# One-level Strassen products for the mLSTM branch and the output projection of a hybrid mLSTM / attention layer

## The chip, the cores and the metric

The kernel runs on one core of a Trainium2 chip. TensorE (PE in the profile) multiplies matrices, VectorE (DVE) and ScalarE (ACT) do element work and read its results from PSUM, GpSimd (POOL) does element work between SBUF tiles, and SyncE's queue (SP) issues most of the DMAs. The metric is the device time of one execution in microseconds (us), the median of several runs. Lower is better.

## The reference

One layer of a diffusion backbone in float32, with 1024 latent tokens of width 1024 and 256 context tokens. Two token mixers work on the same modulated input: windowed attention and a bidirectional mLSTM. Their outputs `att` and `ml` (1024x1024 each) are merged, projected and added to the input; a convolutional feed-forward network (FFN) follows. The part that the change touches:

```python
def merge_branches(att, ml, ga_pre, gm_pre, w_branch_att, w_branch_ml, w_out):
    y = jax.nn.sigmoid(ga_pre) * (att @ w_branch_att) + jax.nn.sigmoid(gm_pre) * (ml @ w_branch_ml)
    return y @ w_out
...
    acc = conv_b
    for j in range(CONV_W):
        acc = acc + up[:, j:j + L] * conv_w[j]
    a, g = jnp.split(acc, 2, axis=-1)
    return (jax.nn.silu(g) * a) @ w_down
```

There are three products of 1024x1024 by 1024x1024 here: the attention branch, the mLSTM branch and the output projection. Behind the projection stand a gated residual, a norm, and the up projection `h @ w_up` of the FFN.

## The kernel before

**Precision.** Every float32 matrix product is made of three fast passes. An operand `x` is split into a high part (a copy to `float32r`, on ScalarE) and a low part (`x - high`, on VectorE); `split_from` (line 47) does both. `mm3` (line 85) and `product` (line 1897) then issue high x high, high x low and low x high for each block of 128 along the contraction. A tile of 128x512 of a 1024-deep product is so 8 x 3 = 24 matmuls of 512 columns.

**Stages.** `layer_kernel` (line 100) runs the startup, the attention with its gate projections (`stage_attention`, line 518), the mLSTM (`stage_mlstm`, line 906), and the tail (`stage_tail`, line 1583), which calls `stage_ffn` (line 2018).

**The order.** In the attention and the mLSTM the order of the instructions is written out by hand. `Pinned` (line 494) chains the instructions of each of PE, DVE, ACT and POOL in the order in which they are emitted; all of them show line 504 in the profile. `ORDER_CORE` (line 885) is a string in which each letter takes the next step of one generator in `stage_mlstm`: for instance `m` is a step of the output gates, `D` and `O` are state updates and outputs, `N` loads an operand of the attention branch, `X` and `Z` make its high and low parts, `Y` is one block of its product (3 matmuls), and `l` multiplies a finished tile by its gate. Half of the attention branch (8 of 16 tiles, 64 `Y`) is done here, in `att_step` (line 1544). In the tail nothing is pinned: the framework's scheduler orders each engine's instructions by their place in the program and by what is ready in its own model of time.

**The tail.** In this order:

- the other 8 tiles of the attention branch (`ya`), with the loads and splits of `mT`, the mLSTM's output, beside them (`ml_load`, `ml_split`, lines 1666 and 1671); gated results go to `y1_d` in DRAM
- the mLSTM branch: 16 tiles `ym` of 24 matmuls. Each is multiplied by its gate (line 1711), the attention branch is added (line 1712), and the sum `y` is split for the next product. Beside them run 16 of the 64 steps of the modulation (`mod_product`, line 201, and `mod_row`, line 223; the first 48 ran in the attention stage, at one or two per block of queries)
- the output projection: 16 tiles `op` in `project` (line 1734), added into the residual `acc` on VectorE. `weight_sums` (line 1815) makes the first 5 of 11 sums of the down projection's weights on VectorE beside it. With the projection's second half the input of the up projection is made: squares and factors of the norm, `first_half` (line 1773) transposes the first 512 tokens, and `pair_sums` (line 1786) makes Strassen operands from the others
- the up and the down projection as Strassen products already, in units (`Units`, line 1906) and in 7 products

GpSimd has only the norm factors to do in the tail. PSUM has 8 banks, in pools with tags, of which the next free one is given.

Of the kernel before, what the change touches and what calls it, by code (L numbers as in the profile page):

```python
# [8 lines left out]
F32 = mybir.dt.float32  # L9
# [90 lines left out]
def layer_kernel(ctx: ExitStack, tc: tile.TileContext, A: dict, out: bass.AP, dbg=None):  # L100
# [25 lines left out]
    ps1 = psx.enter_context(tc.tile_pool(name="ps_mm", bufs=2, space=PSUM, reuse_waits="tile"))  # L126
    pst = psx.enter_context(tc.tile_pool(name="ps_tp", bufs=3, space=PSUM, reuse_waits="tile"))
# [10 lines left out]
    def mm_tile(name):  # L138
        return ps1.tile([P, 512], F32, tag="mm", name=name)

    def fl_tile(name):
        return ps1.tile([P, 512], F32, tag="fl", name=name, bufs=1)

    def tp_tile(name):
        return pst.tile([P, 512], F32, tag="tp", name=name)

    def s_tile(name):
# [6 lines left out]
        nc=nc, tc=tc, A=A, ident=ident, expo=expo, vecT=vecT, mods=mods, m2=m2, g_d=g_d, wmod={}, maccs={}, rows=[], hT=hT, gtile=gtile, gb=gb, dr=dr, out=out,  # L154
        attT_d=attT_d, mlT_d=mlT_d, sga_d=sga_d, sgm_d=sgm_d, kx_d=kx_d, vx_d=vx_d, sil3=sil, sil=sil[:, :, 0], dbg=dbg,
        mm_tile=mm_tile, fl_tile=fl_tile, tp_tile=tp_tile, s_tile=s_tile, psx_s=psx_s,
# [21 lines left out]
    E.ph1, E.sX = ph1, ExitStack()  # L178
    with ExitStack() as st:
        stage_mlstm(E, st)  # L180
    if "mlT" in dbg:
        dump(nc, tc, mlT_d, dbg["mlT"])
# [6 lines left out]
    E.sX.close()  # L189
# [11 lines left out]
def mod_product(E, pool, n):  # L201


    nc, (i, k) = E.nc, divmod(n, KT)
    q, o = i // 2, i % 2 * 4
    if k == 0:
        E.macc = pool.tile([P, 512], F32, tag="macc", name=f"macc{i}", bufs=1 if q < 3 else 2)
        E.maccs[i] = E.macc
    ws, bufs = E.wmod, 1 if q < 3 else 3
    for m in range(n, min(n + bufs, 48 if q < 3 else 64)):  # L210
        if m not in ws:
            ws[m] = pool.tile([P, 512], F32, tag="wmod", name=f"wmb{m}", bufs=bufs)
            nc.sync.dma_start(ws[m], E.A["w_modB"][m // KT][:, m % KT])
    w = ws.pop(n)
# [4 lines left out]
    if k == KT - 1 and q < 3:  # L219
        E.rows.append(i)  # L220


def mod_row(E, pool, i):
# [8 lines left out]
    if i in (1, 7):  # L232
        pg = E.tp_tile(f"gT{q}")
        nc.tensor.transpose(pg[:KT, :P], E.m2[:, 0], E.ident)
        row = pool.tile([P, 512], F32, tag="wmod", name=f"grow{q}", bufs=1 if q < 3 else 3)[:KT, :P]
        nc.vector.tensor_copy(row, pg[:KT, :P])
        nc.sync.dma_start(E.g_d[q // 3].rearrange("o (k c) -> (o k) c", c=P), row)
# [280 lines left out]
def stage_attention(E, st, at):  # L518
# [306 lines left out]
    for n in range(N + 6):  # L825
        a, s, c, x, y = [Bs.get(n - d) for d in (0, 1, 3, 4, 5)]
        quota = (0, 0, 4)[n] if n < 3 else (7 if n < N else 10)
        for step in ORDER if n < N else ORDER_END:
# [37 lines left out]
            elif step == "p" and n < N and mods.n < 3 * (n + 1) // 2:  # L866
# [19 lines left out]
    "vEvvvEvevvUvUvuEvuKvVveEwvvvUKAvuvVvBAvevwBqqKVqeqwwqwAqkkBHDDHmcUqzUqAzqcQuquyqqBqqqqSSQSSymmsmmsmhmmhSaSMSaSEmmsmmsh"  # L886
    "EmDeDammUcmUcmh1mumCu1mMaEmCmdemdmmEmDMDemcUmcUmumCmumCdOeIdOmmfmmMgmGmmDFIDcUmfmcUmMumCgmCmOdFIdOumfmmgmmMmFImDfDmcUm"
    "gUmCmcmFmMdOCuIAuOdmfmBmmAmgmvMBDFGIDUcvfcUvCuvCgvAvdFOdIBODfDuUvgUvAcvFcKIVuvCuvfwvCdvgvdvFBvvKvVvwvOIO1vf1vgvviIvKrv"
    "fvpVDgDvUiUvRvcvwvCcvuKdOVIuCO1wvfd1vgvviIvrvfpvgDDKVvUiUvRvcvwCcvuvCdvuOdIO1vf1xvgKvVviIwvrvfpvgvvivRKvVvwAOIO1xBvf1v"
    "AgvvivBIrqKfpqVqgAqRqwBqTiTwtqPwrqrPqrqprqtqpRQqApqyqRpRqBPkQkRPmHmyTHzPmmtzmTPSStSSSSsSSsmhmsmhmamMmhsmEmamhmamEmaemm"  # L890
    "mEDDmcmcUmMmUemuEmummmMmemDDmcUemcUmu1mum1mCmMmdGmmmDDmcUmCUmuMmdCmcmOdIMuOCmfmdmgmmmDFIDcUmfmcUCmgmMmCdOAFIuOdmfBmmAm"
    "gmvMBDGFIDUcvfUcvCuvCgvAvdFOuIBODfDdUvgUvAcvFcIKVvuCuvfwvCdvgvvdFvuBvKvVOwIOvfvgvvFIvfvDgDKVvUcUvwFvCcvuCvdOuIdO1vf1vg"
    "vviKIVvfwvDgDvUiUvcvcvCuCvudOIKdVO1vfw1vgvviIvfvDgDvUiUvcvcKvVuvCuCwvdOIdO1vf1xvgvviIvKVvfwvAgvviAOBIO1xvfB1vvgqKiVqwI"
    "rPqwrwqprqrpqARkpfmRmrBmprmDRrpDRqHgpqAqipQzTrTRUqtRUqRtpyqPcqRqcPuquBqPkQTPTHyStSSzStmmsSSsShSmhammsmMEmsmhmamhmameED"
    "aDmcmUmcmUmu1mMum1CmECmdmMmdemEDDmcemcmUmUmumCuOMIdGOmmmmmmfDCDgMmUmeUmcmFdIcmmuOummfmCmgMmCmDdFIdOUcDfmumUCgmmmdmMFcI"
    "OAummfmBCmmAmgvMDBGDFIUOcUvdvcvfuvuAgvCDBDCFIOUdfUvcvgAvdvKFVcICOuvfwCvdvgvdvFuIBvfvKvgVvwOFIO1vf1vgvviIvrvfpDKDVgvUvi"
    "UvRvcvwCcvuOCdIO1uvfd1vgKvVviIwvrvfpDDgvUviUvRvcKvcVuvCwCOdIO1dvfuvgvviIvrvfpvKVgvvivRvwvvOIKVOvfwvgvAviIvABvrvBfvpqgK"
    "VqRqwqiqrPqApTrTBkrPDrRDqpctcqHpqRtzqpQRqUyqURqPuuqPqqPkQTTHyStSSzStmmsSSsShSmhammsmNmsDhDamUhmUcmMNmcmCumCamDdDNmUcmU"
    "amnCmdMINdOOfcmnumCgImbmufDFdDumUcmbUmgOMmCcmFIdOCumfumdDDgmUmUcmFIcOMumfumCmgCmDdDFIcOUdmfUmcCmgmCmmMdFIuOdmfmnuDgDnm"
    "UcmUIcFOCumfumnCdmbmgnmMDbdDFIcUOcmfmuCmgCmbmmdbFIdOMmfDDgmmmimcIOcCmmfdCNgXXNiIMZNOXZfNZXYNgXYXNiYXZNIXOdYNfZXYZNXYgY"  # L900
    "NXiYXZIOZNYXZfYNZXYNgYNiYXZINXOZYfNZYXngYXYniXZIOXZYfZYbgYbYiIZrYZrYNplrYNlrpYfRYprlrYRprgYXYpRXYRpiYZrTpZTNtYpRtYNRRY"
    "RYZYXZTXZTYtlYtZYYYlYYYYYYYYlYYYYYYYYlYYYYYYYl"
# [3 lines left out]
def stage_mlstm(E, st):  # L906
# [5 lines left out]
    psd = E.psx_s.enter_context(tc.tile_pool(name="ps_d", bufs=2, space=PSUM, reuse_waits="tile"))  # L912
# [11 lines left out]
    zz = mp.tile([P, P], F32, name="zz")  # L924
    nc.gpsimd.memset(zz, 0.0)
    ones = mp.tile([P, P], F32, name="onesm")
    nc.gpsimd.memset(ones, 1.0)
# [3 lines left out]
    def gate_math():  # L931
        with ExitStack() as s2:
# [4 lines left out]

            lf = gp.tile([P, NBLK, 8], F32, name="lf")
# [384 lines left out]
    def update():  # L1323
        for h, d, i in STEPS:
            c = chunk(d, i)
            (kh, kl), (vh, vl) = kw.pop((h, d, i)), V[h, c]
            dC[h, d, i] = pd = psd.tile([P, 512], F32, tag="d", name=f"dC{h}_{d}_{i}")
# [158 lines left out]
    E.y1_d = dr.tile([D, L], F32, name="y1_d")  # L1486
    E.aT, E.wba = [[], []], []
    araw, ag, psy = {}, {}, {}

    def x512(pool, name, dt=F32R):  # L1490
        return E.xts[pool].tile([P, 512], dt, tag="x", name=name)

    def att_load():
        for q in range(24):
            k, a = (q // 2, q % 2) if q < 16 else (q - 16, 2)
            if q == 4:
                E.ph1.close()
                E.xts = [E.sX.enter_context(tc.tile_pool(name=f"xt{i}", bufs=8, reuse_waits="tile")) for i in range(6)]
            if q < 4 or q >= 16:
                raw = wp.tile([P, 4, P], F32, tag="ub", name=f"ar{q}", bufs=4).rearrange("p c t -> p (c t)")  # L1500
            else:
                raw = x512(5, f"ar{q}", F32)
            if a == 0:
                nc.sync.dma_start(raw, A["w_ba"][0][:, k])
            else:
                nc.sync.dma_start(raw, E.attT_d[0][k * P : (k + 1) * P, (a - 1) * 512 : a * 512])
            araw[q] = raw
            yield

    def att_high():  # L1510
        for q in range(24):
            k, a = (q // 2, q % 2) if q < 16 else (q - 16, 2)
            to = E.wba if a == 0 else E.aT[a - 1]
            pool_ = ((3, 4), (0, 1), (2, 5))[a][k // 4]
            to.append([x512(pool_, f"a{a}{x}{k}") for x in "hl"])
            copy(to[-1][0], araw[q])
            yield

    def att_low():
        for q in range(24):  # L1520
            k, a = (q // 2, q % 2) if q < 16 else (q - 16, 2)
            hi, lo = (E.wba if a == 0 else E.aT[a - 1])[k]
            sub(lo, araw.pop(q), hi)
            yield

    def att_place(c):
        return sl(c % 4 * P, P), sl(c // 4 * 512, 512)

    def att_gate_load():
        for c in range(8):  # L1530
            if c % 2 == 0:
                i = bs.take(("g", c // 2), 2)
                for j, x in enumerate("hl"):
                    ag[c + j] = bp.tile([P, 512], F32, tag=f"b{x}{i}", name=f"sga{c + j}")
            rs, ts = att_place(c)
            nc.sync.dma_start(ag[c], E.sga_d[rs, ts])
            yield

    def att_gate():
        for c in range(8):  # L1540
            act.activation(ag[c], ag[c], AF.Sigmoid)
            yield

    def att_step():
        for k, c in [(k, c) for k in range(KT) for c in range(3)] + [(k, c) for c in range(3, 8) for k in range(KT)]:
            if k == 0:
                psy[c] = bk.take(("y", c), f"ya{c}")
            mm3_step(psy[c], cols(E.wba[k], sl(c % 4 * P, P)), E.aT[c // 4][k], k == 0, k == KT - 1)
            yield

    def att_out():
        for c in range(8):
# [745 lines left out]
```

## Time and profile before

| what | us |
|---|---|
| runs shown: median of 3 | 1937.71 |
| lowest and highest | 1933.21, 1939.3 |
| the profiled execution's own time | 1932.65 |
| its span, first to last instruction | 1930.6 |
| first matmul of the attention branch, from the start | 1005.0 |
| first matmul of the mLSTM branch | 1101.8 |
| first matmul of the output projection | 1196.8 |
| first matmul of the up projection | 1292.7 |

The page begins with the busy time of each engine and its share of the span. A digit in its 40 slices is the busy share in tenths. In a view by windows, a row gives the window, its length, then for each engine the busy time and the number of instructions, then the granted share of TensorE's clock, the busy share of the DMA engines and GB/s. In a view of one tile, a row gives an operation, how often it ran, its shortest, median and longest time in ns, and when the first and the last one started. In a timeline, the first number is the start and the second the duration, both in us. Matmuls overlap in TensorE, so that a row's duration is longer than the time from one start to the next.

### The profile page before, as it was taken

The numbers are of one execution on the slowest core, as the hardware profiler recorded it, in microseconds if no ns is written. First come the engines' busy times: TensorE is split into PE (matmuls) and PEld (weight loads), VectorE is DVE, ScalarE is ACT, GpSimd is POOL, SyncE is SP. The second block draws the span as 40 slices with busy tenths as digits, with TensorE's granted clock in tenths as the row PEclk, the third lists the DMA queues.
The fourth block names the chain that finished last, engine by engine and source line by source line (L and its number), as shares of the span: only waits on it lengthen the run. The fifth ranks groups of instructions, "written<-read, shape, count | busy, mean of one in ns | idle before, by whom it ended". The sixth has DMA issues, their size and how long they took to land.

```text
span 1930.6 us, 28360 instructions
## 1 busy us (share of the span) xinstructions
PE 1902.0 (99%) x10108; PEld 1644.5 (85%) x10108; DVE 1352.8 (70%) x2642; ACT 963.4 (50%) x1897; POOL 346.9 (18%) x594
## 2 busy tenths in 40 slices
PE   8999999999999999999999999999999999999998
PEld 3988888888888899999997787887888888888887
DVE  2877767777776456666585467369878898895564
ACT  4856556556556354646354322256545444465441
POOL 1333333333333133434321000010000000000000
PEclk9999999999999999999999999999999999999999
DMA  8723223223222321413238667622244544499641
GB/s 313 231 93 94 77 66 104 72 77 91 80 67 74 103 62 51 117 49 99 55 122 277 219 201 238 231 88 81 94 151 187 196 153 174 164 326 326 230 164 66
DMA packets 134062, 273.34 MB, mean 142 GB/s; under 512 B 14736, under 2 KB 47136, under 8 KB 130592
## 3 DMA queue, kind: packets, MB, share of 16 engines
q1 hardware_dynamic: 127392, 256.85, 40.1%
q10 hardware_dynamic: 5760, 10.49, 1.7%
q0 software_dynamic: 768, 4.20, 1.3%
q8 instruction: 79, 1.29, 0.3%
q14 instruction: 63, 0.52, 0.1%
HBM read 201.67 MB, written 74.00 MB: 143 GB/s over the span
## 4 chain that ended last, share of the span: by engine, by line
PE 89%; DVE 4%; DMA 3%; ACT 2%; issue 1%; POOL 1%; SPq 0%; ACTq 0%; POOLq 0%; DVEq 0%
PE g L504 9%; PE kv L504 7%; PE pq L504 6%; PE mo L504 5%; PE pa L1901 4%; PE pa L1902 4%; PE pa L1903 4%; PE s L504 4%; PE po L504 4%; PE pt L504 3%; PE q L504 2%; PE ya L504 2%; PE dx L1901 2%; PE dx L1903 2%; PE dx L1902 2%; PE pb L1901 2%
## 5 line engine op out<-in xcount | busy, mean ns | idle before, releaser
L504 DVE CUSTOM_DVE_ANT_0 P<-s,maskA,nsink 128x640 f32<-128x640 f32 (+1 forms) x112 | 103.5, 924 | 76.8 <-PE s L504 75.2
L504 ACT ACTIVATE P<-P,st 128x640 f32<-128x640 f32 (+1 forms) x128 | 102.4, 800 | 87.9 <-DVE st L504 87.8
L504 ACT ACTIVATE ph<-pt 128x512 fp32r<-128x512 f32 x152 | 90.4, 598 | 60.0 <-PE pt L504 58.4
L504 DVE TENSOR_TENSOR pl<-pt,ph 128x512 fp32r<-128x512 f32 x152 | 101.1, 681 | 25.8 <-ACT ph L504 25.6
L504 POOL TENSOR_SCALAR P<-P,st 128x640 f32<-128x640 f32 (+1 forms) x128 | 110.9, 886 | 32.0 <-DVE st L504 11.1
L504 PE MATMUL g<-hH,fh 128*128 128x512 f32 x256 | 106.5, 416 | 0.2 <-ACT fo L504 0.2
L504 PE MATMUL g<-hH,fl 128*128 128x512 f32 x256 | 100.9, 394 | 0.0
L504 PE MATMUL g<-hL,fh 128*128 128x512 f32 x256 | 100.8, 394 | 0.0
L504 PE MATMUL pt<-ident,P 128*128 128x128 f32 x608 | 90.9, 272 | 0.5 <-DVE m L504 0.5
L504 PE MATMUL pq<-w1h,hH 128*128 128x384 f32 (+1 forms) x256 | 87.1, 340 | 0.0
L504 PE MATMUL kv<-w1h,hH 128*128 128x384 f32 x256 | 86.9, 340 | 0.0
L504 PE MATMUL pq<-w1l,hH 128*128 128x384 f32 (+1 forms) x256 | 86.9, 339 | 0.0
L504 PE MATMUL pq<-w1h,hL 128*128 128x384 f32 (+1 forms) x256 | 86.5, 338 | 0.0
L504 PE MATMUL kv<-w1h,hL 128*128 128x384 f32 x256 | 86.1, 336 | 0.0
L504 PE MATMUL kv<-w1l,hH 128*128 128x384 f32 x256 | 86.1, 336 | 0.0
L504 PEld LDWEIGHTS pt<-ident,P 128*128 128x128 f32 x608 | 75.4, 140 | 12.2 <-DVE m L504 0.7
L504 PE MATMUL mo<-w1h,hH 128*128 128x256 f32 x256 | 72.5, 283 | 0.0
L504 POOL TENSOR_SCALAR ss<-ss 128x5 f32<-128x5 f32 x64 | 13.2, 206 | 327.1 <-DVE ss L504 324.1
L504 PE MATMUL mo<-w1h,hL 128*128 128x256 f32 x256 | 71.8, 281 | 0.0
L504 PE MATMUL mo<-w1l,hH 128*128 128x256 f32 x256 | 71.7, 280 | 0.0
L49 DVE TENSOR_TENSOR dfl<-drf,dfh 128x512 fp32r<-128x512 f32 x55 | 38.0, 691 | 46.1 <-ACT dfh L44 46.1
L2039 ACT ACTIVATE cv<-ua,vecT 128x1024 f32<-128x1024 f32 x22 | 27.4, 1245 | 85.5 <-DVE ua L2012 85.5
(581 smaller groups left out, 6346.6 us busy)
## 6 DMA issues: line engine op xcount, KB each, us to landing
ur<-in_w_up SPq DMA_DIRECT2D x22, 1024.0 KB, 5.0
wmb<-in_w_modB SPq DMA_DIRECT2D x64, 256.0 KB, 2.8
f_d<-cv SPq DMA_DIRECT2D x22, 512.0 KB, 2.7
wm<-in_w_modA SPq DMA_DIRECT2D x16, 512.0 KB, 8.2
fr<-in_w_g SPq DMA_DIRECT2D x32, 256.0 KB, 2.7
drf<-fs_d SPq DMA_DIRECT2D x15, 512.0 KB, 5.8
drw<-wt_d SPq DMA_DIRECT2D x14, 512.0 KB, 5.6
w1b<-in_w_cx SPq DMA_DIRECT2D x16, 388.0 KB, 5.1
```

The source lines that it names most:

```text
L49: (nc.vector if eng == "v" else nc.gpsimd).tensor_tensor(lo, src, hi.bitcast(F32), op=ALU.subtract)
L504: i = f(*a, **k)
L1901: nc.tensor.matmul(ps, lh, rh, start=start and i == 0, stop=False, skip_group_check=True)
L1902: nc.tensor.matmul(ps, lh, rl, start=False, stop=False, skip_group_check=True)
L1903: nc.tensor.matmul(ps, ll, rh, start=False, stop=stop and i == n - 1, skip_group_check=True)
L2039: nc.scalar.activation(r, u, AF.Identity, bias=vecT[:, V_CB + ch : V_CB + ch + 1], scale=cw(1))
```

## The change

The mLSTM branch and the output projection become Strassen products: both matrices are cut into quadrants of 512x512, and 7 products of half size, of sums and differences of quadrants, take the place of 8. All three merges, and the up projection up to its first unit's first matmuls, are put in the written order: `stage_tail` starts behind them.

- `merge_steps` makes lists of steps under letters, and `ORDER_CORE` and the new string `ORDER_MERGE` take them in turn. A product step `5` is 6 matmuls (2 blocks of the contraction, one bank of 128x512); 4 banks and 2 steps each make one of the 7 products. The attention branch keeps its plain form (`Y`, 128 steps, 46 of them in `ORDER_CORE`).
- Operands are held in tiles of 128x1024 (`Gen`: a list of slots in three pools). `2` loads one, `X` makes a high part (ScalarE), `Z` a low part (VectorE), `4` a sum on GpSimd, a backquote a sum on VectorE, `3` scales a weight of the output projection by the residual's gate (VectorE).
- Partial results move from PSUM to `U` and `U4` tiles (`#` on ScalarE; `$`, `%`, `(`, `)`, `*` on VectorE), are gated (`9`, VectorE) and added to the attention branch (`~`, now on GpSimd). In the output projection, `&` adds such a tile into the residual on GpSimd and `^`, `(`, `)`, `*` add the last product from PSUM on VectorE.
- The first five weight sums (`[` loads, `]` sums) go from VectorE to GpSimd.
- The 16 late modulation steps go into the attention stage, at two per block instead of one or two.
- All loads of the stage go through SP's queue; gates and `y1` went through ScalarE's before.
- PSUM banks are named one by one (`bank`) instead of given by pools, and `lead` no longer splits the first up unit.

The core of the diff:

```diff
-            elif step == "p" and n < N and mods.n < 3 * (n + 1) // 2:
+            elif step == "p" and n < N and mods.n < min(2 * (n + 1), 64):
...
+ORDER_MERGE = (
+    "8888YY27YlY2YY2YXY2YZXY6Y2lXYZY6XY2ZY7Y2ZXYY27YZYX2lYYZX6Y2YZXY2YZY72YlY`6YYYY4Y7YlYY64Y`YYY7YYlYY6XYY2ZYYX2YY7l2YZY2Y"
+    "Y`6YYYY4lY7Y6YY4Y`Y7YYlYY6YYYY7YYlYY6XY2YXZY2YZ7Y25lX25ZX652ZX45`75[ZX45`#52Z#45`#5`#2X3542Z5352]35X2]35Z]5$4X5$$5ZX[]"
+    "5$Z52X35]Z5]X[35X9]Z5]9529]XZ5[X]95Z~5Z~563X8]536X85ZX]7%5~X%5Z7~6%58X]%[Z5]67Z58X]Z5]Z75X]5X(Z]5X(X5]X9(5](Z5~Z569458"
+    "995Z75~Z5)~6)589~6)58)~67589467589579~57~5`68~5`685*4X6`85X0Z757Z075*0`50*5X*0X95Z0~#5Z05909~#59#5#~X5~XZ5ZX45X`5XZ45Z"
...
+SUMS = dict(m="DPPDPDDP", o="DPDPPDPP")
+YADD = "PPPP"
...
+    def split(key, src, last):
+        def high():
+            h = gs.tile((key, "h"), nm(key) + "h")
+            T[key] = h, gs.tile((key, "l"), nm(key) + "l")
+            act.activation(h, T[src], AF.Copy)
+
+        def low():
+            dve.tensor_tensor(T[key][1], T[src], T[key][0].bitcast(F32), op=ALU.subtract)
...
+    def summ(q, i, out, a, b, alu, rel=()):
+        eng = SUMS[q][i]
+        op("4" if eng == "P" else "`", lambda: (pool if eng == "P" else dve).tensor_tensor(T[out], T[a], T[b], op=alu), rel)
...
+    def wsum(k, j):
+        (a0, a1), (b0, b1) = [[T["w", k, x][:, i * 512 : (i + 1) * 512] for i in range(2)] for x in range(2)]
+        o, a, b = ((a0, a1, a0), (a1, b1, a1), (b1, b1, a0), (b0, b0, b1))[j]
+        pool.tensor_tensor(o, a, b, op=ALU.subtract)
...
+    OPS = {1: ("A11", "B11"), 6: ("S2", "T2"), 2: ("A12", "B21"), 5: ("S1", "T1"), 7: ("S3", "T3"), 3: ("S4", "B22"), 4: ("A22", "T4")}
...
+        def prod(p, banks, start):
+            def step(z, c):
+                if start and z == 0:
+                    ps[q, p, c] = E.bank(banks[c], f"{q}p{p}_{c}")
+                o = ps[q, p if start else {2: 1, 3: 5, 4: 7}[p], c]
+                a, b = [T[q, "p" + x, z] for x in OPS[p]]
+                lhs, rhs = [part(a, kk, sl(c * P, P)) for kk in Z2], [part(b, kk, full) for kk in Z2]
+                product(fixed, o, lhs, rhs, start and z == 0, z == 1)
...
+        def pre(b, h, u):
+            pool.tensor_tensor(acc[b][:, h], acc[b][:, h], u(), op=ALU.add)
...
-            dv = nc.vector.tensor_tensor(sg, ps, sg, op=ALU.mult)
-            nc.vector.tensor_tensor(sg, sg, y1, op=ALU.add)
...
+                (dve if YADD[c] == "D" else pool).tensor_tensor(o, sg.pop(key), y1.pop(key), op=ALU.add)
...
     scale(4)
-    U.lead(0)
     U.prep_apart(0, lambda n, dt=F32R: x512(n, dt, 1))
     scale(5)
-    first_half(H)
-    project(1, 6, w)
-    square(6)
     fa = [op2(f"fa{k}", F32) for k in range(H)]
     for k in range(H):
         pair_sums(0, k, fa[k])
```

The seven products of a gemm run in the order 1, 6, 2, 5, 7, 3, 4 (the projection: 3 before 7). The last lines of `ORDER_MERGE`, not shown, hold the end of the projection, the norm of the residual, the transposes of the first 512 tokens and the first matmuls of the up projection (4 steps of 6).

More of the change, by code (lines that the diff above doesn't have):

```diff
@@ L1871, in stage_tail @@
         t3(0, k)
-    U.lead(1)
-    U.first_mm(0)
+    U.mid[0] = E.first[0], E.first[1]
     scale(7)
```

738 lines of the change are left out of this document (459 added, 279 removed).

## The prediction

> **What bounds the kernel now.** I read the page first, then busy time by windows over the tail, then the list of waits of TensorE, then single tiles.
>
> ```profile
> span 1930.6 us, 28360 instructions
> ...
> PE 1902.0 (99%) x10108; PEld 1644.5 (85%) x10108; DVE 1352.8 (70%) x2642; ACT 963.4 (50%) x1897; POOL 346.9 (18%) x594
> ...
> PE   8999999999999999999999999999999999999998
> ```
>
> TensorE is busy from end to end, so only fewer matmuls or fewer gaps can shorten the span. The means of the matmul rows (0.39 us) overlap one another and must not be added up; what one matmul costs is read from a stretch that holds nothing else:
>
> ```profile
> core 0: us, PE busy (x) PEld busy (x) DVE busy (x) ACT busy (x) POOL busy (x), PEclk, DMA share, GB/s
> 1056.00:1102.00 46.00, 44.03 (x193) 35.82 (x192) 18.74 (x25) 12.69 (x21) 0.00 (x0) 1.00 0.65 217
> 1102.00:1146.00 44.00, 43.78 (x191) 35.42 (x190) 26.57 (x39) 16.04 (x25) 0.00 (x0) 1.00 0.60 191
> 1146.00:1196.00 50.00, 47.29 (x204) 38.12 (x203) 36.00 (x54) 10.33 (x16) 0.00 (x0) 0.97 0.72 242
> 1196.00:1243.00 47.00, 44.85 (x202) 36.55 (x201) 24.16 (x32) 12.13 (x22) 0.00 (x0) 1.00 0.66 237
> ...
> 1300.00:1330.00 30.00, 29.74 (x137) 24.16 (x136) 29.74 (x63) 23.28 (x49) 0.00 (x0) 1.00 0.18 61
> 1400.00:1500.00 100.00, 100.00 (x443) 82.81 (x442) 84.81 (x100) 48.21 (x59) 0.00 (x0) 1.00 0.47 170
> ```
>
> In 1400 to 1500 us, 443 matmuls of 512 columns take 100 us: 0.2257 us each. Note the POOL column: GpSimd does nothing in the tail today.
>
> ```profile
> L90 PE MATMUL ya<-a1h,wba1h x32: 387/389/395, 1055.7 to 1079.3; 128*128 128x512 f32 x32
> ...
> L92 PE MATMUL op<-wo0h,yl x64: 387/389/477, 1197.3 to 1243.0; 128*128 128x512 f32 x64
> ```
>
> From 1055.7 to 1243.2 us run half of the attention branch, the whole mLSTM branch and half of the output projection: 192+384+192 = 768 matmuls. They need 173.4 us, with some 2 us for the small matmuls of the modulation (the third window's surplus over 192), and took 187.5. So about 12 us are lost there. The waits name most of it:
>
> ```profile
> PE ym L90 <- DVE sgm L1711: 2.7, 2, 2.4
> PE ya L92 <- DVE wba1l L49: 2.0, 2, 1.5
> PE gT L234 <- DVE m L229: 1.6, 1, 1.6
> PE x2p L1791 <- DVE acc L1755: 0.9, 1, 0.9
> PE ya L504 <- DVE a1l L504: 0.9, 1, 0.9
> ```
>
> (us in total, times, longest.) All end on VectorE. Just outside the stretch lie 1.8 us more, the last two rows.
>
> **The change part by part.** *Matmuls.* The mLSTM branch and the output projection are 16 tiles of 24 matmuls each, 768 in all. As Strassen products each is 7 products of 4x4x3 = 48, 336, so 672 in all. 96 fewer at 0.2257 us: **-21.7 us**. The attention branch, the mLSTM scans and the FFN keep theirs.
>
> *Old gaps.* The loops in which they arose are gone: **-13 us** (12 of the stretch, 1 of its edges) if nothing takes their place. That is the next question.
>
> *Element work.* Strassen's price is paid on other engines. Seven pairs of operands per matrix product must be split into high and low parts instead of the plain operands: 28 copies on ScalarE and 28 subtractions on VectorE of 128x1024 per product, where the plain form needs 16. There are 16 sums of 128x1024 per product, 14 of the 32 on VectorE and 18 on GpSimd. The addition of the attention branch (16 of 128x512), the first five weight sums of the FFN (20) and 12 additions into the residual are put on GpSimd. Durations:
>
> ```profile
> L49 DVE TENSOR_TENSOR wbm1l<-wbm1r,wbm1h 128x1024 fp32r<-128x1024 f32 x4 | 4.9, 1223 | 2.6 <-ACT wbm1h L44 2.6
> ...
> L1712 DVE TENSOR_TENSOR sgm<-sgm,y 128x512 f32<-128x512 f32 x16 | 11.0, 687 | 0.0
> ```
>
> ```profile
> L504 POOL TENSOR_TENSOR qf<-qf,t x32: 858/880/888, 106.3 to 583.3; 128x320 f32<-128x320 f32 x32
> ```
>
> ```profile
> L504 POOL TENSOR_TENSOR ub<-ub,mlmask x16: 1282/1296/1484, 671.4 to 891.0; 128x512 f32<-128x512 f32 x16
> ```
>
> The line through 320 columns (0.88) and 512 (1.30) gives 2.4 us for 1024 on GpSimd; bounds are 1.3 (no more than 512 columns) and 2.6 (twice that). I take 2.4. ScalarE stays far below its limit and hides its 24 extra copies. VectorE and GpSimd each fit into the time too, counted apart. But they do not run apart:
>
> ```profile
> 291.29 0.88 POOL L504 TENSOR_TENSOR qf<-qf,t 128x320 f32<-128x320 f32 x1
> ```
>
> ```profile
> 291.47 0.73 DVE L504 TENSOR_TENSOR st<-st 128x4 f32<-128x4 f32 x1 [0.39 <-ACT P L504]
> 292.23 0.18 DVE L504 RECIPROCAL st<-st 128x4 f32<-128x4 f32 x1
> ```
>
> An addition of four columns, worth the 0.18 us of its neighbour, starts inside a GpSimd addition and ends only with it, after 0.73 us. And:
>
> ```profile
> 798.23 1.32 POOL L504 TENSOR_TENSOR ub<-ub,mlmask 128x512 f32<-128x512 f32 x1
> ```
>
> ```profile
> 797.94 1.76 DVE L504 SCALAR_TENSOR_TENSOR kwl<-k,gcall,kwh 128x128 fp32r<-128x128 f32 x2 [3.29 <-POOL kwh L504]
> ```
>
> ```profile
> L504 DVE SCALAR_TENSOR_TENSOR kwl<-k,gcall,kwh x72: 333/345/1381, 674.3 to 997.5; 128x128 fp32r<-128x128 f32 x72
> ```
>
> The second of two 0.345 us operations lasts 1.38 us, until GpSimd is done. A VectorE operation with two inputs in SBUF and a GpSimd addition exclude one another. One with an input in PSUM does not wait: here `pl` takes its usual 0.68 us inside a GpSimd stretch of 3.31.
>
> ```profile
> 292.61 3.31 POOL L504 TENSOR_SCALAR P<-P,st 128x640 f32<-128x640 f32 x3 [0.43 <-PE s L504]
> ```
>
> ```profile
> 294.48 0.68 DVE L504 TENSOR_TENSOR pl<-pt,ph 128x512 fp32r<-128x512 f32 x1
> ```
>
> [...]
>
> *The sum under exclusion.* I count the letters of the new order from the third of its 112 product steps to the 94th, in the fifth product of the output projection. These are 91 steps of 6 matmuls, 91 x 1.354 = 123 us of TensorE. In them stand 46 low parts, 10 VectorE sums and 8 gate scalings (64 of 1024 columns, both inputs in SBUF), 12 gate products with both inputs in SBUF (512), and on GpSimd 14 sums of 1024 and 46 operations of 512. Because the lead of one operation overlaps the one before it (the held one above ends 0.15 us after GpSimd, not 0.345), I count 1.1, 0.57, 2.3 and 1.15 us. 70+7+32+53 = 162 us must pass one after the other beside 123 us of TensorE: 39 us too many. Another 37 VectorE operations with an input in PSUM (22 us) can lie under GpSimd's. What softens it is how far ahead of their use the results are ordered. Low parts stand four to eight product steps ahead and most sums eight to fifteen; I take nine steps, 12 us, as what the order absorbs. That leaves **+27 us** of new waits of TensorE on low parts. Bounds: 3 (if the order leaves room for nearly all; a few single waits as in the rows above stay) and 49 (the 22 us do not overlap either, 39+22-12).
>
> *The hand-over to the up projection.* Today VectorE is busy 29.74 of 30 us from 1300 to 1330, and TensorE is just fed. The operand sums of the up projection's first unit (scales, `prep_apart`, the first `pair_sums`) lie beside three of the last projections today; after the change the tail's code begins when the last of them is done. That moves these to the end:
>
> ```profile
> 1288.30 0.42 DVE L1784 TENSOR_TENSOR acc<-acc,g1b 128x256 f32<-128x256 f32 x1
> 1288.64 0.42 DVE L1784 TENSOR_TENSOR acc<-fa,acc 128x256 f32<-128x256 f32 x1
> ```
>
> 16 subtractions and 4 low parts at 0.34 us from start to start, 6.7 us, with six operations of 512 columns, about 4: 11 us moved, against 24+24 matmuls of first products (10.8 us) that stay as cover but are also there today. I take **+4 us**, between 0 and 11.
>
> *The rest.* Sixteen modulation products (0.74 us of VectorE each) and two row groups move into the attention stage.
>
> ```profile
> L504 DVE SCALAR_TENSOR_TENSOR macc<-wmb,sil,macc x42: 741/745/753, 108.0 to 582.3; 128x512 f32<-128x512 f32 x42
> ...
> 400.00:500.00 100.00, 99.75 (x583) 89.54 (x581) 77.36 (x179) 60.22 (x138) 36.55 (x48) 1.00 0.31 88
> ```
>
> 12 us over 32 blocks of 16 us on an engine that is 77% busy: hidden; without that cover 12. The wait of `gT` (1.6 us) moves with them. All loads now go through SP's queue, which waits in order for tiles to come free; a load that is held holds the gate and weight loads behind it. The mLSTM order changes without new work. For all of this **+1 us**, from 0 to 12.
>
> Sum: -21.7 -13 +27 +4 +1 = **-3 us**. The profiled execution took 1932.65 us (span 1930.6); the median of the runs shown is 1937.71, 5 us above it. I set the difference against the median: **1935 us**. A difference of 0.3% (6 us) is about what a measurement of this kernel can tell from none.
>
> **The rivals.** *A, my forecast:* exclusion costs 27 us, within ten either way: 1925 to 1945. For it: the two held operations and the written pattern, about one 1.30 us GpSimd and one 1.22 us VectorE operation to every 1.354 us step. *B, half of it:* GpSimd falls behind VectorE and its results (the weight sums above all, which TensorE needs only in the down projection) come late without harm; 12 us remain: -18, 1920 us. For it: most sums stand eight steps ahead. Against: GpSimd works in order, and the additions that make the output projection's operands stand behind those weight sums. *C, the order holds:* 3 us of waits remain, -27, 1911 us. For it: each engine alone has time. Against: the 0.73 us row. *D, slower:* VectorE's operations from PSUM do not slip under GpSimd's, because VectorE works in order and stands at a held operation before them. Then 49 us: +19, 1957 us. It decides as soon as a held low part stands ahead of an operation that frees PSUM. For it: the order puts `%`, `(` and `*` right behind low parts. Against: `pl` above ran freely.
>
> [...] In 1146 to 1196 us one gap of 2.4 us goes with a granted 0.97; longer gaps would add to D, which no run here shows yet.
>
> **How the numbers follow.** A 0.45, B 0.2, C 0.17, D 0.18. Faster by over 0.3% (below 1932): C, nearly all of B, a third of A: 0.17+0.18+0.13 = 0.48. Within: over half of A and a little of B: 0.27. Slower (above 1943.5): nearly all of D and an eighth of A: 0.25. A's own range is 1925 to 1945. The range over all cases runs from 1909, which leaves out half of C, to 1952, which leaves out half of D and some: 0.2 outside.
>
> **What would show it.** Matmul count lower by 96 at 0.2257 us each: right or wrong at once. Exclusion: low parts of 128x1024 well over 1.22 us and GpSimd sums over 2.4 where they overlap, and TensorE waiting on `l` tiles of the Strassen operands, some 27 us in the list of waits. If these rows are as short as alone, C holds. If TensorE waits most on PSUM banks, it is D. For the hand-over: waits at the first `t2` and `t3` products. The forecast is wrong if the order leaves more room than nine steps, or if a held load on SP's queue leads the list of waits.

## The result: slower, and the profile after

The changed kernel takes 1965.47 us (median of 4 runs, 1963.04 to 1968.59), the kernel before 1936.66 us (4 runs beside them): a ratio of 1.0151 with a 95% interval from 1.0128 to 1.0173. The forecast was 1935 us, and its range ended at 1952.

The page of the changed kernel, its span, its busy times and the slices of TensorE and of its clock:

```profile
span 1961.0 us, 28302 instructions
...
PE 1899.5 (97%) x10012; PEld 1638.6 (84%) x10012; DVE 1446.8 (74%) x2641; ACT 993.7 (51%) x1902; POOL 495.6 (25%) x660
...
PE   8999999999999999999999987798999999999999
...
PEclk9999999999999999999999989899999999999999
```

96 matmuls are gone, as forecast. But TensorE, which was filled from end to end before, has 7 or 8 tenths in four of the slices 24 to 28 (each is 49 us), and its granted clock is lower in two of them. The windows of that stretch have as columns the busy time and the number of instructions of each engine, then the granted clock:

```profile
core 0: us, PE busy (x) PEld busy (x) DVE busy (x) ACT busy (x) POOL busy (x), PEclk, DMA share, GB/s
...
1090.00:1140.00 50.00, 50.00 (x223) 41.39 (x222) 32.09 (x20) 15.35 (x20) 23.51 (x9) 1.00 0.62 210
1140.00:1180.00 40.00, 30.34 (x118) 23.75 (x117) 32.13 (x28) 9.45 (x10) 25.27 (x15) 0.87 0.68 230
...
1200.00:1220.00 20.00, 13.23 (x50) 10.47 (x49) 19.97 (x14) 3.16 (x5) 19.25 (x10) 0.83 0.55 179
```

From 1090 to 1140 TensorE runs without a gap: 223 matmuls in 50 us. From 1200 to 1220 it does 50 in 20 us, where 89 would fit. VectorE is busy for all of those 20 us and yet completes 14 instructions, GpSimd 10. Two engines look full while little gets done: their operations wait inside themselves (low parts, 1.22 us alone, take up to 2.66 in the mean in the groups below). The list of what TensorE waits for (total, times, longest, in us), cut to the merges and what follows them:

```profile
PE op L516 <- DVE u4wm L516: 6.8, 1, 6.8
PE mp L516 <- DVE m_pT_1l L516: 5.8, 1, 5.8
PE op L516 <- DVE o_pT_0l L516: 5.2, 2, 3.1
...
PE mp L516 <- DVE um L516: 3.5, 1, 3.5
PE op L516 <- ACT o_pA_0h L516: 2.9, 1, 2.9
...
PE ya L516 <- ACT pa_w_0h L516: 2.5, 1, 2.5
PE pa L2163 <- DVE q2l L49: 2.5, 1, 2.5
PE pa L2161 <- ACT t2h L44: 2.2, 1, 2.2
PE op L516 <- DVE o_pB_1l L516: 2.1, 1, 2.1
PE op L516 <- DVE uo L516: 1.8, 1, 1.8
...
PE op L516 <- DVE o_pB_0l L516: 1.5, 1, 1.5
```

Names that end in `l` are low parts; `um`, `u4wm` and `uo` are the sums that VectorE makes of a PSUM bank. The groups of instructions from 1060 to 1320 us, shapes kept apart (busy time, then mean ns of one):

```profile
L516 POOL TENSOR_TENSOR ws<-ws 128x512 f32<-128x512 f32 x10 | 20.0, 2007 | 7.7 <-DMA ws<-in_w_dn 7.4
...
L516 POOL TENSOR_TENSOR o_B<-o_B,o_B 128x1024 f32<-128x1024 f32 x6 | 18.9, 3142 | 5.8 <-DVE o_B L516 5.8
...
L516 DVE TENSOR_TENSOR o_pB_1l<-o_B,o_pB_1h 128x1024 fp32r<-128x1024 f32 x3 | 8.0, 2659 | 0.0
...
L516 DVE TENSOR_TENSOR sgm<-u4pm,sgm 128x512 f32<-128x512 f32 x4 | 7.4, 1893 | 0.0
...
L516 DVE TENSOR_TENSOR m_pT_1l<-m_B,m_pT_1h 128x1024 fp32r<-128x1024 f32 x4 | 6.8, 1692 | 7.9 <-DMA wt_d<-ws 7.9
...
L516 DVE TENSOR_TENSOR um<-mp,um 128x512 f32<-128x512 f32 x8 | 5.2, 680 | 0.0
...
L516 POOL TENSOR_TENSOR m_B<-m_B,m_B 128x1024 f32<-128x1024 f32 x2 | 4.8, 2389 | 48.1 <-DMA m_B<-mlT_d 34.6 <-DMA y_d<-sga 13.5
```

This is the exclusion of the forecast. Low parts, 1.22 us alone, have means up to 2.66 here; the gate product with two inputs in SBUF (`sgm<-u4pm,sgm`) takes 1.89 us, while the sum with one input in PSUM (`um<-mp,um`) keeps its 0.68. On GpSimd a sum of 1024 columns grows from 2.39 (`m_B`, the two that ran undisturbed) to 3.14.

To add losses up I use one measure throughout: from the trace, the time from the start of a matmul to the start of the next, less the median of that time for matmuls of the same width, summed. In microseconds, with the waits (single steps of over 0.45 us too long) and the matmuls at about half clock (0.427 us from start to start in the changed kernel's trace, where the others have 0.227) told apart:

| stretch | before | after | of it waits | half clock |
|---|---|---|---|---|
| attention branch, from 1000 us | 4.5 | 9.3 | 4.9 | 3.3 |
| mLSTM and output products | 9.3 | 46.6 | 33.5 | 11.7 |
| hand-over, 60 us from the first `x2p` | 2.6 | 10.8 | 6.0 | 4.0 |

The rows grow by 4.8, 37.3 and 8.2 us; less 21.7 for the matmuls that is 28.6. The spans differ by 1961.0 - 1930.6 = 30.4, so 1.8 us lie elsewhere: ahead of 1000 us, where the same measure gives 26.3 before and 28.2 after.

### The profile page after: what moved, and what is told of

It reads as the page before. It is cut to its first block, busy times and chain, and to the rows that moved or that the text cites. A ratio compares the mean times of both kernels' runs of the same rounds, so it can differ in the third digit from the quotient of the medians.

```text
span 1961.0 us, 28302 instructions
## 1 busy us (share of the span) xinstructions
PE 1899.5 (97%) x10012; PEld 1638.6 (84%) x10012; DVE 1446.8 (74%) x2641; ACT 993.7 (51%) x1902; POOL 495.6 (25%) x660
## 4 chain that ended last, share of the span: by engine, by line
PE 83%; DVE 6%; DMA 4%; issue 2%; ACT 2%; POOL 2%; SPq 0%; DVEq 0%; ACTq 0%; POOLq 0%
PE g L516 8%; PE kv L516 7%; PE pq L516 6%; PE pa L2163 4%; PE pa L2162 4%; PE pa L2161 4%; PE mo L516 4%; PE s L516 4%; PE po L516 3%; PE pt L516 3%; PE ya L516 3%; PE op L516 2%; PE q L516 2%; PE pb L2163 2%; PE dx L2162 2%
## 5 line engine op out<-in xcount | busy, mean ns | idle before, releaser
L516 POOL TENSOR_SCALAR P<-P,st 128x640 f32<-128x640 f32 (+1 forms) x128 | 110.5, 882 | 31.5 <-ACT ph L516 10.9
L44 ACT ACTIVATE dfh<-drf 128x512 fp32r<-128x512 f32 x55 | 34.5, 630 | 69.1 <-PE dy L2162 34.1
```

The source lines that it names most:

```text
L44: nc.scalar.activation(out, in_, AF.Copy, scale=scale)
L516: i = f(*a, **k)
```

## Experiments

Theory T is the forecast's: what passes in turn on VectorE and GpSimd is more than TensorE covers. Its rivals are R1, VectorE alone has too much to do in this order; R2, the FFN's weight sums, made early, hold tiles that the splits wait for; and for the last 10.8 us the hand-over. R2 has a row above: VectorE stood idle for 7.9 us ahead of `m_pT_1l` until the store `wt_d<-ws` was done. For most variants one window is shown, from the first matmul of the mLSTM product to the first transpose of the hand-over: the same some 730 matmuls each time, so its length alone is the comparison. In the changed kernel it is 208 us:

```profile
1111.00:1319.00 208.00, 176.43 (x729) 140.65 (x728) 186.34 (x149) 85.94 (x125) 146.25 (x78) 0.93 0.49 170
```

**The two engines by themselves, and gaps of TensorE.**

```diff
+    for _ in range(12):          # dve: do = da - db, pool: po = pa + pb
+        low(1024)
+        add(1024)
...
+    for i in range(40):
+        pe.matmul(bank, wr, mr, start=i == 0, stop=i == 39)
+    act.activation(ao[:, h], bank, AF.Copy)
+    for _ in range(n - 1):
+        act.activation(ao[:, h], ao[:, h], AF.Copy)
```

> Only measured rows, none of the layer is computed: subtractions on VectorE and additions on GpSimd of 512 and 1024 columns alone, then both at once, then VectorE with one input in PSUM and with a single input in SBUF beside GpSimd, then bursts of 40 matmuls with gaps between them. Theory T: alone 0.69 and 1.22 us on VectorE, 1.3 and 2.4 on GpSimd; at once they take turns, so that twelve of each last 12 x (1.2+2.4) = 43 us and a mean of either grows to about 3.5 us; with an input in PSUM 0.68 us as alone. Rival (no exclusion, only a slower port for both): both stretch by the same share and overlap, 29 to 35 us for twelve of each. Of the gaps: matmuls after a gap of more than about 2.5 us take 0.43 us for 8 to 15 instructions, after shorter ones 0.226.

The timeline of VectorE in the first 60 us, each engine alone (start, length, engine; consecutive equal instructions in one row; in brackets the idle time before and what ended it):

```profile
25.62 0.15 DVE L109 COPY da<-po 128x1 f32<-128x1 f32 x1 [7.89 <-POOL po L109]
...
26.07 7.52 DVE L109 TENSOR_TENSOR do<-da,db 128x1024 f32<-128x1024 f32 x6
...
48.43 0.15 DVE L109 COPY da<-po 128x1 f32<-128x1 f32 x1 [14.34 <-POOL po L109]
...
53.10 4.70 DVE L109 TENSOR_SCALAR do<-da,db 128x1024 f32<-128x1024 f32 x6
```

VectorE waits 7.89 us for six additions of 512 columns on GpSimd and 14.34 for six of 1024. The timeline of both engines after that:

```profile
58.34 39.34 DVE L109 TENSOR_TENSOR do<-da,db 128x1024 f32<-128x1024 f32 x12
...
98.63 26.00 DVE L109 TENSOR_TENSOR do<-da,db 128x1024 f32<-128x1024 f32 x12
...
125.06 21.70 DVE L109 TENSOR_TENSOR do<-pv,db 128x512 f32<-128x512 f32 x30
125.37 24.16 POOL L109 TENSOR_TENSOR po<-pa,pb 128x1024 f32<-128x1024 f32 x10 [0.42 <-POOL pa L109]
...
150.01 43.22 DVE L109 TENSOR_SCALAR do<-da,db 128x1024 f32<-128x1024 f32 x30
...
197.09 0.69 DVE L109 TENSOR_TENSOR do<-pv,db 128x512 f32<-128x512 f32 x1
197.81 2.52 DVE L109 TENSOR_TENSOR do<-da,db 128x1024 f32<-128x1024 f32 x1
```

Twelve subtractions beside twelve additions of 1024 columns last 39.34 us, 3.28 for a pair; beside additions of 512, 26.00, 2.17 for a pair. Alone a subtraction takes 7.52 / 6 = 1.25 us, GpSimd's additions 14.34 / 6 = 2.39 and 7.89 / 6 = 1.31. So a pair costs the sum of both less 0.36 to 0.4: they take turns. The 43 us expected for twelve pairs were 4 too many, the rival's 29 to 35 too few. With one input in PSUM, 30 operations take 21.70 us, 0.72 each, as alone, and GpSimd's ten take 24.16, also as alone. The last two rows show them alternating: the one from PSUM runs inside GpSimd's addition in 0.69, and the next with two SBUF inputs stands until GpSimd is done, 2.52. The unit prices of the forecast were nearly right (2.3 + 1.1 = 3.4 for the pair).

The same run has bursts of 40 matmuls with gaps between them. The windows of the first 3.4 us after gaps with waits of 1.35, 2.07, 2.73 and 4.71 us (1.74, 2.46, 3.12 and 5.10 from start to start):

```profile
252.30:255.70 3.40, 3.37 (x15) 2.80 (x16) 0.00 (x0) 0.00 (x0) 0.00 (x0) 1.00 0.00 0
263.75:267.15 3.40, 3.40 (x8) 2.69 (x9) 0.00 (x0) 0.00 (x0) 0.00 (x0) 0.53 0.03 5
277.45:280.85 3.40, 3.39 (x8) 2.74 (x9) 0.00 (x0) 0.00 (x0) 0.00 (x0) 0.52 0.00 0
307.30:310.70 3.40, 3.40 (x8) 2.72 (x9) 0.00 (x0) 0.00 (x0) 0.00 (x0) 0.50 0.02 5
```

After the short gap 15 matmuls start in 3.4 us at full clock, after each longer one 8 at half. In this run the 11 waits of 2.07 us or more cost another 1.5 to 2.4 us each (the starts of the next 21 matmuls against 0.227 us each), the two of 1.4 us nothing; the limit of 2.5 us that was expected is too high.

**GpSimd's additions made small.**

```diff
-        pool.tensor_tensor(o, a, b, op=ALU.subtract)
+        pool.tensor_tensor(o[:, :32], a[:, :32], b[:, :32], op=ALU.subtract)
```

(and likewise for the other three kinds; for the sum of the two branches ScalarE copies the gated part over first, 16 copies more).

> All of GpSimd's additions of the merges stay where they are, with their waits, but work on 32 columns only (what is left out is the sum over the other columns; for the sum of the two branches ScalarE copies the gated mLSTM part over instead, 16 copies of 512 columns). Theory T: the exclusion goes, VectorE's own 100 us fit beside 123 us of TensorE: the gaps between 1090 and 1280 us nearly all go, 1905 to 1922 us. Rival R1: VectorE's load is unchanged, 1955 to 1968 us. Rival R2: as T. Whatever the hand-over to the up projection costs (10.8 us were lost from 1320 to 1360) stays under each of them.

1917.92 us, a ratio to before of 0.9916 (0.9895 to 0.9937): some 47 us below the changed kernel. The window of the products, and two groups of VectorE in it:

```profile
1115.00:1279.00 164.00, 162.57 (x730) 133.63 (x729) 128.84 (x147) 92.20 (x138) 59.29 (x78) 1.00 0.61 211
```

```profile
L516 DVE TENSOR_TENSOR o_pB_1l<-o_B,o_pB_1h 128x1024 fp32r<-128x1024 f32 x3 | 3.7, 1235 | 0.0
...
L516 DVE TENSOR_TENSOR sgm<-u4pm,sgm 128x512 f32<-128x512 f32 x4 | 2.6, 694 | 0.0
```

208 us become 164 at full clock, with VectorE's own work unchanged in its number of operations. These are back at the prices that they have alone (1.24 us for 2.66, 0.69 for 1.89), and VectorE's busy time falls from 186 to 129 us. R1 in its plain form is out: VectorE alone, with the order and all of its waits, fits. Two other things go with the exclusion here: the store of R2 holds VectorE no longer, and GpSimd's results come earlier. The second is small where VectorE itself is concerned: of its 22 us of idle time in the changed kernel's window, 3 end on GpSimd. ScalarE waits there 16 us for two of its sums; what that adds is not shown. The hand-over still loses 10.8 us here, so it is not the exclusion's doing.

**Without the early weight sums.**

```diff
-    for k in range(5):
+    for k in range(0):
         op("[", lambda k=k: wsum_load(k))
...
-    E.w_early = 5
+    E.w_early = 0
```

> The five weight sums of the FFN (20 subtractions of 512 columns on GpSimd, with their loads and stores) are taken out of the merges and made by VectorE in the FFN loop, as before the change. The rest is the changed kernel (1965 us). Theory T, GpSimd's additions and VectorE's operations with two inputs in SBUF exclude one another: of the 162 us that must pass in turn beside 123 us of TensorE, 23 go, 16 are too many instead of 39; the gaps shrink by about 23 us and their half clock with them: 1930 to 1942 us. Rival R1, VectorE itself is over its capacity in the new order: nothing leaves VectorE in that stretch, 1960 to 1968 us. Rival R2, the late weight sums hold tiles that the loads and splits of the output projection wait for: nearly all of the 46 us between 1140 and 1280 go, 1915 to 1927 us.

1947.57 us (1945.41 to 1948.63), 18 us below the changed kernel, 1.0064 (1.0047 to 1.0082) of before:

```profile
1113.00:1303.00 190.00, 171.55 (x730) 137.20 (x729) 174.79 (x149) 85.43 (x125) 107.66 (x58) 0.96 0.38 134
```

By R1 nothing would have changed; R2 alone would have given some 45 us. T has the sign, but 1930 to 1942 was too hopeful: 23 us of work in turn less gave 18, and 28.6 us are still lost in this stretch where 4 were expected.

**Everything on VectorE.**

```diff
-        pool.tensor_tensor(o, a, b, op=ALU.subtract)
+        dve.tensor_tensor(o, a, b, op=ALU.subtract)
```

(and likewise the sums, the additions of the branches and into the residual).

> Order, loads and stores as in the changed kernel, but all of GpSimd's additions of the merges run on VectorE (14 sums of 1024 columns counted from the third product step to the 94th, and 46 operations of 512). Theory T: nothing is left to exclude, VectorE alone has about 77+42+22 = 141 us of work beside 123 us of TensorE, 18 too many instead of 39: faster than the changed kernel, 1935 to 1948 us. Rival R1: VectorE, already the bound, has 42 us more to do: slower than the changed kernel by 20 to 40 us, 1985 to 2005 us. Rival R2: the weight sums are made in 0.6 us each instead of 1.3 to 2, the tiles come free: 1935 to 1950 us, which does not tell it from T.

1949.22 us (1943.46 to 1952.79):

```profile
1114.00:1305.00 191.00, 172.40 (x734) 137.48 (x733) 174.28 (x212) 86.48 (x125) 12.63 (x16) 0.96 0.53 185
```

VectorE has taken over GpSimd's work, completes 212 instructions where it completed 149, is busy for less time (174 us against 186), and the stretch is 17 us shorter. Nothing shows more plainly that GpSimd's help costs VectorE more than the work itself. The time is just above the upper end of T's range, and far from R1's 1985. R2's range, 1935 to 1950, holds it too: by its time alone this run doesn't tell T from R2.

**The sums on VectorE, or everything, both without the early weight sums.**

```diff
-        op("4" ..., lambda: (pool if eng == "P" else dve).tensor_tensor(T[out], T[a], T[b], op=alu), rel)
+        op("4" ..., lambda: dve.tensor_tensor(T[out], T[a], T[b], op=alu), rel)
```

> As the run without the early weight sums (1947.6 us), and the 18 Strassen sums of 1024 columns that GpSimd made are made by VectorE; GpSimd keeps the additions of the two branches and into the residual. The rows by themselves showed a pair of 1024 and 1024 columns at 3.28 us in turn, against 2.51 for two operations on VectorE. Theory T (what counts is the time in turn): 14 x 2.3 become 14 x 1.1, 139 us of work in turn become 122, beside 123 us of TensorE: 1930 to 1940 us. Rival R1 (VectorE's own load counts): VectorE gets 17 us more than in the run without early weight sums: 1950 to 1960 us.

> As the run with everything on VectorE (1949.2 us), and without the early weight sums: GpSimd makes none of the merges' additions. Theory T: VectorE's 141 us become 130, 7 too many beside 123 us of TensorE, which the lead of the order can absorb: 1934 to 1944 us, since about 11 us of its waits go. Rival R2 (the weight sums harm by their tiles and loads, not by the time that they take): more than 20 us go, below 1929 us. Rival R1: as T.

1930.32 us (0.9986 of before, 0.9976 to 0.9995) and 1929.38 us (0.9979, 0.9967 to 0.9991). The first with the 28 additions of 512 columns that GpSimd keeps, the second without:

```profile
1109.00:1287.00 178.00, 167.54 (x729) 135.28 (x728) 163.54 (x163) 85.89 (x125) 66.92 (x43) 0.98 0.40 138
```

```profile
1110.00:1284.00 174.00, 166.47 (x727) 135.12 (x727) 161.85 (x191) 85.05 (x124) 11.77 (x16) 0.98 0.40 139
```

The first lies in T's range and 20 us below R1's. In the second 11 us of work less brought 20 us, between the two expectations: the tiles and stores of the weight sums (R2) may have a part of it, which these runs don't separate.

**Other matmuls as cover for the hand-over.**

```diff
     U.first_ev(0)
+    U.lead_first(2)
     put_t1(1)
...
     U.first_ev(1)
+    U.first_mm(2)
     U.prep2_apart(0)
-    U.lead_first(2)
...
-            U.first_mm(2)
```

> The changed kernel (1965 us), with the first products of the up projection's third unit (48 matmuls, 10.8 us) moved ahead of the first unit's remaining products, and their weight's split with them. Theory of the hand-over: VectorE and ScalarE have some 13 us of operand work there, whose cover, the last output projections, is gone; 10.8 us of other matmuls as cover take the waits of 2.4, 0.9 and 2.7 us and the half clock after them away: 6 to 10 us faster than the changed kernel, 1955 to 1959 us, and the waits on t2h and q2l are gone. Rival: the split of that weight is itself late, since it stands on the same two engines, so that the wait moves to it: 1962 to 1968 us.

1965.22 us, no change, as the rival has it. Waits of TensorE after 1320 us:

```profile
PE pa L2162 <- ACT t2h L44: 2.2, 1, 2.2
PE pa L2162 <- ACT q1h L44: 2.1, 1, 2.1
...
PE pa L2164 <- DVE q1l L49: 0.7, 1, 0.7
```

The wait on `q2l` is gone, but one on the next unit's `q1` stands in its place; the loss is 10.9 us as before. Cover borrowed from a later unit seems to be paid back there, since the work on VectorE and ScalarE is the same. Together with the sums on VectorE and without the early weight sums:

> The sums on VectorE, no early weight sums, and the early first products together. If the two effects add: 1935 less 6 to 10, 1924 to 1932 us, a little below the kernel before. Rival (hand-over split late): no better than the run with the sums on VectorE alone.

1932.17 us (1928.0 to 1936.38), no better than the 1930.32 without it: the rival.

**Less work in the hand-over.**

```diff
-        sub(b21, b21, t2r[:, k])
...
     def t3(g, k):
-        sub(f[:, cols[0]], f[:, cols[1]], f[:, cols[0]])
+        pass
```

> The changed kernel (1965 us) without 16 of the subtractions of 256 columns on VectorE in the hand-over (left out: those that make t3 and the raw form of t4; their tiles keep the old values, and the split of them stays). ScalarE's work there is unchanged. If VectorE's amount of work sets the hand-over, 16 x 0.34 = 5.5 us of it go and with them the half clock after the gap that closes: 5 to 9 us faster, 1956 to 1960 us, and the wait on q2l (2.5) is gone or near it. Rival, ScalarE sets it (the waits on t2h and fa end on ScalarE): 1962 to 1968 us with both waits as before.

1965.92 us. The hand-over's loss fell from 10.8 to 8.4 us, and the wait on `q2l` is gone; but the products lost more in the profiled execution (51.4 against 46.6), so the total says nothing, and neither expectation held: the time is in the rival's range, the wait on `q2l` went as in the other. 5.5 us less on VectorE gave 2.4. The windows of the hand-over in the changed kernel show why neither engine can be named alone:

```profile
1320.00:1330.00 10.00, 8.81 (x49) 6.43 (x47) 9.90 (x28) 8.95 (x23) 0.00 (x0) 1.00 0.01 3
1330.00:1340.00 10.00, 8.14 (x26) 5.67 (x26) 9.95 (x29) 9.12 (x24) 0.00 (x0) 0.83 0.00 1
```

VectorE is busy for 19.85 of 20 us, ScalarE for 18.07. Which of the two decides stays open.

**Adding by DMA, and a better order.** In the run with everything on VectorE and no early weight sums, ScalarE shows this row:

```profile
1226.47 0.63 ACT L516 ACTIVATE xj<-acc 128x512 f32<-128x512 f32 x1 [10.13 <-DVE acc L516]
```

Ten microseconds idle before a square that waits for VectorE, with four splits of operands queued behind it. Two variants start from that kernel. The first lets the transfer of the attention branch add it to the gated mLSTM part:

```diff
+                dve.tensor_tensor(T["o", quad, c // 2][:, c % 2 * 512 : c % 2 * 512 + 512], get(), sg[key], op=ALU.mult)
...
+                pool.dma_start(T["o", quad, c // 2][:, c % 2 * 512 : c % 2 * 512 + 512], E.y1_d[rs, ts], accum_op=ALU.add)
...
-                (dve if YADD[c] == "D" else pool).tensor_tensor(o, sg.pop(key), y1.pop(key), op=ALU.add)
+                pass
```

> As the run with everything on VectorE and no early weight sums (1929.4 us), and the attention branch is added to the gated mLSTM part by the DMA as it loads it (16 transfers that accumulate, issued by GpSimd's queue) in place of 16 additions of 512 columns on VectorE. Theory (VectorE's time in the stretch, 130 us beside 123 of TensorE, is what is left): 16 x 0.69 = 11 us go, it fits: of the 13 us still lost between 1180 and 1260 most go, 1916 to 1924 us. Rival: a transfer lands some us after its issue, and the operands of the output projection, which wait for it, come later than the addition would give them: 1929 to 1940 us, with waits on o operands that end on the DMA.

The second keeps these transfers and moves that square and four of the additions into the residual back in the order (two passages of the string, before and after):

```diff
-^5o^4X5^χ5ZX^&5XZ5&XZ5ψ&ZX5Z&X5ZX5Zoo5
+^5^4X5^χ5ZX^5XZ5XZ5ψZX5ZX5ZXo5Zoo5
...
-α5oWα5Wα5&α5ζ5(5o(
+α5&oWα5&Wα5&α5&ζ5(5&o(
```

> As the run with the adding transfers (1928 us), with five letters of the fixed order moved and no work changed: the first four additions into the residual stand 16 to 18 product steps later, and the first square on ScalarE, behind which that engine stood idle for 10.25 us with splits queued, eight steps later. Theory: between 1210 and 1240 VectorE is full and in order, so what is put ahead of the splits makes them late: 4 x 0.69 us less ahead of them and ScalarE free: the waits of 3.4 us on o_pA_1h and 1.2 on o_pT_1l shrink by about 3, with up to 2 us of half clock: 1922 to 1926 us. Rival: the splits wait for VectorE's sums anyway, and the residual's additions are late in the hand-over instead: 1927 to 1932 us.

1927.95 us (0.9973 of before, 0.9962 to 0.9984) and 1926.24 us (1919.76 to 1930.93; 0.9957, 0.9944 to 0.997). The last is faster than both kernels, by 0.43% than the one before, and by 39 us than the change. Whether it is faster than the first of the two is not clear: the intervals of their ratios overlap. Its window, in an execution with a span of 1928.8 us:

```profile
1115.00:1287.00 172.00, 165.16 (x730) 134.48 (x729) 151.88 (x175) 85.81 (x125) 27.06 (x32) 0.99 0.45 129
```

The adding transfers gave 1.4 us, which is within the noise of the two runs, where 5 to 13 were expected: with 11 us less to do on VectorE the stretch stayed at 174 us, and TensorE's longest wait there, 3.4 us, ended on a high part of ScalarE. The order gave 1.7 us more, within the noise too and just short of the 2 to 6 that were expected; the stretch is 2 us shorter.

## Why the prediction was wrong

The forecast was 3 us less than before, the spans give 30.4 more. Of the 33 us between them 20 belong to the exclusion, 4 to the hand-over and 9 to the old gaps and the rest.

*Matmuls, -21.7:* right. 10012 instead of 10108, and 223 in 50 us where nothing waits.

*Old gaps, -13:* half right. Their loops are gone, but the attention branch kept its waits and got worse, from 4.5 to 9.3 us (2.5 on `pa_w_0h` and 14 matmuls at half clock after it). The part called "the rest", +1, within 0 and 12, should have held these 4.8 and the 1.8 from ahead of 1000 us.

*Exclusion, +27, between 3 and 49:* the mechanism is shown, by the rows of the two engines alone and by the run with small additions (47 us faster). The size failed, at 46.6: 33.5 us of waits and 11.7 of half clock. Of the 19.6 us by which the term is short, 6.5 are waits and 11.7 half clock, so two steps of the sum failed: what the order absorbs, and the clock (below). The first is this one: "I take nine steps, 12 us, as what the order absorbs." Set the work in turn that I count from the letters against what the 730 matmuls took beyond the 164 us of the run with small additions:

| variant | work in turn, us (beside 123) | beyond 164 us |
|---|---|---|
| small additions | 100 | 0 |
| all on VectorE but the branch additions, which the DMA makes, no early weight sums | 119 | 10 |
| sums on VectorE, no early weight sums | 122 | 14 |
| all on VectorE, no early weight sums | 130 | 10 |
| no early weight sums | 139 | 26 |
| all on VectorE | 141 | 27 |
| the change | 162 | 44 |

The loss doesn't begin 12 us above TensorE's 123 us, as I assumed, but somewhere between 100 and 119, and over the whole table it grows by some 0.7 us for each. The figures aren't all of one kind: in the rows with small additions and with all on VectorE the 22 us of operations from PSUM are counted in, in the other three they count as lying under GpSimd's (with them these would be 144, 161 and 184). The rows with all on VectorE are free of that choice, since GpSimd adds nothing there. With 12 us absorbed, their 119, 130 and 141 us should have lost 0, 0 and 6; they lost 10, 10 and 27, half clock included. A likely reason is that the work isn't spread evenly over the steps: where VectorE is full for 20 us on end, the lead is used up, and what it could do in a slack window is not ready yet. A sum over 123 us treats slack and peaks as exchangeable. That is read from the windows; it wasn't varied by itself, but for the five letters moved in the last run.

*The clock, at nothing in the sum:* 11.7 of the 46.6 us, and some 16 us over the three stretches (19.0 against 3.0), are matmuls at about half clock behind the waits. The forecast saw one gap of 2.4 us go with a granted 0.97 and priced longer gaps only as an addition to D. The run with the bursts gave half clock after a wait of 2.07 us (0.53 granted over the next 3.4 us). Without this, 33.5 us of waits stood against 27, well inside the case's "within ten".

*Hand-over, +4, from 0 to 11:* it rose by 8.2 us, from 2.6 to 10.8, and did so in every variant (9.0 to 10.9, or 8.4 with work left out). The term was mis-sized: 8.2 of the 11 us moved came to bear, some 3 of them as half clock, and matmuls put in as cover gave nothing.

*The rivals.* D's 1957 us came nearest, and its mechanism is there in part: the waits on `u4wm`, `um` and `uo` (6.8, 3.5 and 1.8 us in the trace) are for operations that read PSUM and take 0.68 us themselves. The timeline of VectorE before the longest:

```profile
1197.93 6.25 DVE L516 TENSOR_TENSOR sgm<-u4pm,sgm 128x512 f32<-128x512 f32 x3
1204.11 2.28 DVE L516 TENSOR_TENSOR o_pA_1l<-yA,o_pA_1h 128x1024 fp32r<-128x1024 f32 x1
1206.31 2.28 DVE L516 TENSOR_TENSOR o_pB_1l<-o_B,o_pB_1h 128x1024 fp32r<-128x1024 f32 x1
1208.51 1.28 DVE L516 TENSOR_TENSOR u4wm<-mp,um 128x512 f32<-128x512 f32 x2
```

Three gate products of 0.69 and two low parts of 1.22 us, each drawn out by GpSimd, take 10.5 us, and `u4wm` stands behind them. The four waits on low parts in the list (5.8, 5.2, 2.1 and 1.5) make 14.6 us, these three 12.1. So D isn't ruled out as a part of the loss, and no run separates its part. B counted on GpSimd's lateness doing no harm; but the store of the first weight sums already held VectorE for 7.9 us at `m_pT_1l`, and the 5.8 us that TensorE waited for it came that way, which is R2's.

## What to carry to other kernels

Work given to GpSimd to relieve VectorE was no relief here, where both read two tiles from SBUF: price such a pair as one queue, here 3.28 us for two operations of 1024 columns, against 2.51 for both on VectorE. In a fixed order keep that queue well below what TensorE covers (here 100 us of work on VectorE beside 123 fitted, 119 didn't), and price a wait of over 2 us with the 1.5 to 2.4 us of half clock that stood behind the 11 of 2.07 us or more in the run with the bursts; 8 of the 10 waits of over 2 us from 1000 us on in the changed kernel had half clock behind them too. When matmuls are removed, count what the operations that ran beside them then stand beside.

## What the runs showed beyond that

A single-input operation was not free beside GpSimd either. Six scalings of 1024 columns take 4.70 us alone (the row of 53.10 us above), 0.78 each; the 30 beside ten additions took 43.22 us instead of 23.5. What holds them up is not shown.

The half clock doesn't follow every wait: in the changed kernel a start-to-start gap of 3.91 us at 1143.36 had none behind it. The granted clock in the traces of the two kernels goes with something else. It is recorded as 1.00 or 0.50, and every stretch but the last lasts a whole number of 3.41 us: 3.41 to 10.24 us at half clock, 6.83 to 1174.19 at full. Cut into steps of that length, a trace shows how long TensorE was at work in each. The gap at 1143.36 is divided between two steps, which hold 1.58 and 1.72 us of matmuls, and the clock stays at 1.00. In the run with the bursts, the step from 260.51 us holds 1.34 us, and the next one is granted 0.50. From 60 us on, the two kernels' traces have eleven steps at full clock that half clock follows, with 0 to 1.69 us of matmuls; the steps that full clock follows hold 1.58 us or more. Ahead of the bursts it was otherwise: TensorE did nothing from 235.50 to 238.90 us, and the 9.10 us after that were granted 1.00.
